# Squared distance of rows: a late pair of x and y, row 7 in PSUM, and other load widths at the end of a stream

## Chip, cores, metric

One core of one Trainium2 chip. The metric is device time in microseconds (us) of one execution. Verdicts count a difference from 2%.

## The reference

```python
x, y: (1024, 4096) float32, normal
return np.sum((x - y) ** 2, axis=-1).astype(np.float32)     # 1024 values
```

Two arrays of 16.8 MB are read, and 4 KB are written.

## The kernel before

Each of 128 partitions holds 8 rows of 4096 columns (row 0 to row 7, columns 0 to 32767). SyncE issues a stream of loads of x and y, which alternate and get smaller toward the end. VectorE subtracts a piece as soon as its y has landed (L175), ScalarE squares and sums it (L181), and VectorE adds the sums of the pieces of a row (`complete`, L188). The last 128 columns of row 3 ("late") have their y loaded after all else. VectorE does these alone: it subtracts, then multiplies and sums in one instruction (L204) that starts from the sum of the rest of row 3. So the last landing asks nothing of ScalarE.

```python
xw = [4096, 12288, 8192, 5472, 1280, 960, 320, 160]
yw = [16256, 8192, 2624, 2784, 1344, 480, 480, 288]
late, last = 128, 192
LATE = 3
halved = (1, 2, 3, 4)                     # pieces of these y loads are cut in two
cut = (LATE + 1) * D - late
# ... cut: xs = plain spans of xw; ys = spans of yw, skipping the late columns
ys += [(N - last, N), (cut, cut + late)]

# ... cut: load(), which gives every load its own semaphore
def square(c0, c1, acc):
    a = X[:, home(c0, c1)]
    nc.scalar.wait_ge(diffs, n["diffs"])
    nc.scalar.activation(out=a, in_=a, func=Square, accum_out=acc).then_inc(acts, 1)
    # ... cut: count of squares (other counters are cut below)

for j, (c0, c1) in enumerate(ys):
    final = j == len(ys) - 1
    wait_loaded(c1, landed_y[j][1])
    for piece in pieces_of(j, c0, c1):
        sub(*piece)
        r = piece[0] // D
        if final:
            nc.vector.wait_ge(diffs, n["diffs"])
            nc.vector.tensor_tensor_reduce(
                out=Y[:, home(*piece)], in0=X[:, home(*piece)], in1=X[:, home(*piece)],
                scale=1.0, scalar=parts_of(r, 1), op0=mult, op1=add,
                accum_out=results[:, r : r + 1]).then_inc(sums, 1)
            continue
        square(*piece, where[piece])
        # ... cut: issue of the second half of the loads when rows 0 and 1 are squared
    if j == 4:
        for r in (4, 5, 6):
            complete(r)
complete(7)
nc.sync.wait_ge(sums, n["sums"])
nc.sync.dma_start(out=ov, in_=results).then_inc(stored, 16)
```

## Time and profile before

| | before |
|---|---|
| time, median of 6 runs | 84.13 us (84.0 to 84.2) |
| span of the profiled run | 82.63 us |
| DMA packets, share of 16 engines | 2736, 95.9% |
| last data moved / last two y seen | 79.8 / 80.05 and 80.25 us |
| last reduce starts / store issued | 80.99 / 81.18 us |

The kernel is a stream of 33.55 MB that keeps the DMA engines full from 2 to 79.8 us, with a tail of 1.4 us of work and 1.45 us of store. The page, the windows at the end of the stream, the timeline of the tail and the chain are shown and read in the prediction below.

### The profile page before, as it was taken

Reading aid. Unit: us, or ns where it says so; the run is one execution under the profiler, and the core shown is the slowest. Engines: PE = TensorE matmul, PEld = TensorE weight load, DVE = VectorE, ACT = ScalarE, POOL = GpSimd, SP = SyncE. Lnnn points to the kernel's source line nnn. Section 1 sums busy time; section 2 is a strip of 40 time slices with the busy share of each in tenths; the row PEclk is TensorE's granted clock in tenths of the full one; section 3 lists DMA queues with packets and bytes.
Section 4 is the critical chain, followed back from the end, with each engine's and each line's share of the span. In section 5 each row is a group of like instructions: output and inputs, shape, how many; then the busy total and the mean of one; then the engine's idle time right before and its main releaser. Section 6 shows DMA issues by size and latency. Waiting matters only on the chain.

```text
span 82.6 us, 136 instructions
## 1 busy us (share of the span) xinstructions
DVE 36.8 (45%) x27; ACT 33.4 (40%) x41; POOL 0.2 (0%) x4
## 2 busy tenths in 40 slices
DVE  0000000000000000000299999999189996989992
ACT  3300000000000000000000979889896999899991
POOL 0000000000000000000000000000000000000000
DMA  5998998888999991999599699969979799999960
GB/s 127 389 500 381 595 547 381 381 381 381 504 504 504 504 504 63 441 504 504 254 508 508 286 476 508 476 286 508 423 339 509 339 437 440 426 402 416 395 220 2
DMA packets 2736, 33.56 MB, mean 406 GB/s; under 512 B 432, under 2 KB 1328, under 8 KB 1712
## 3 DMA queue, kind: packets, MB, share of 16 engines
q1 hardware_dynamic: 2736, 33.56, 95.9%
HBM read 33.55 MB, written 0.00 MB: 406 GB/s over the span
## 4 chain that ended last, share of the span: by engine, by line
DMA 63%; SPq 16%; DVE 12%; ACT 4%; issue 1%
DMA Y<-in_y_dram 63%; SPq L108 16%; DVE X L175 11%; ACT X L181 4%; DVE Y L204 0%; DVE results L188 0%; SPq L220 0%; DVE results L204 0%
## 5 line engine op out<-in xcount | busy, mean ns | idle before, releaser
L175 DVE TENSOR_TENSOR X<-X,Y 128x2048 f32<-128x2048 f32 (+10 forms) x21 | 36.2, 1780 | 44.3 <-DMA Y<-in_y_dram 44.3
L181 ACT ACTIVATE X<-X 128x2048 f32<-128x2048 f32 (+9 forms) x20 | 31.2, 1559 | 46.1 <-DVE X L175 46.0
L181 ACT ACTIVATION_READ_ACCUMULATOR X<-X 128x1 f32 x20 | 3.7, 186 | 0.0
L181 ACT ACT_TABLE_LOAD x1 | 1.3, 1283 | 1.4 <-PEq L19 1.4
L188 DVE TENSOR_REDUCE results<-parts 128x1 f32<-128x2 f32 (+2 forms) x4 | 0.4, 152 | 0.0
L204 DVE CUSTOM_DVE_ANT_0 Y<-X,parts 128x128 f32<-128x128 f32 x1 | 0.4, 352 | 0.0
L250 POOL MEMSET const-bfloat16-1.0<- 128x1 bf16 x1 | 0.1, 101 | 0.0
L250 POOL MEMSET const-uint8-127<- 128x1 uint8 x1 | 0.1, 101 | 0.0
L250 POOL MEMSET const-float32-0.0<- 128x1 f32 x1 | 0.1, 98 | 0.2 <-issue 0.2
L250 POOL MEMSET const-float32-1.0<- 128x1 f32 x1 | 0.1, 98 | 0.0
L204 DVE DVE_READ_ACCUMULATOR2_ANT results<- 128x1 f32 x1 | 0.1, 83 | 0.0
## 6 DMA issues: line engine op xcount, KB each, us to landing
Y<-in_y_dram SPq DMA_DIRECT2D x1, 8128.0 KB, 39.0
X<-in_x_dram SPq DMA_DIRECT2D x1, 6144.0 KB, 20.2
X<-in_x_dram SPq DMA_DIRECT2D x1, 4096.0 KB, 48.3
Y<-in_y_dram SPq DMA_DIRECT2D x1, 4096.0 KB, 57.5
X<-in_x_dram SPq DMA_DIRECT2D x1, 2736.0 KB, 13.3
X<-in_x_dram SPq DMA_DIRECT2D x1, 2048.0 KB, 7.1
Y<-in_y_dram SPq DMA_DIRECT2D x1, 1392.0 KB, 19.0
Y<-in_y_dram SPq DMA_DIRECT2D x1, 1312.0 KB, 16.1
```

The lines of the kernel that those rows point to most:

```text
L108: nc.sync.dma_start(out=dst[:, home(c0, c1)], in_=src[:, c0:c1]).then_inc(sem, 16)
L175: nc.vector.tensor_sub(out=a, in0=a, in1=Y[:, home(c0, c1)]).then_inc(diffs, 1)
L181: nc.scalar.activation(out=a, in_=a, func=Square, accum_out=acc).then_inc(acts, 1)
L188: nc.vector.tensor_reduce(out=results[:, r : r + 1], in_=parts_of(r, len(row_parts[r])), axis=mybir.AxisListType.X, op=add,).then_inc(sums, 1)
L204: nc.vector.tensor_tensor_reduce(out=Y[:, home(*piece)], in0=X[:, home(*piece)], in1=X[:, home(*piece)], scale=1.0, scalar=parts_of(r, 1), ...
L250: nc = _bacc.Bacc("TRN2", target_bir_lowering=False, num_devices=1)
```

## The change

It has three parts. The late piece becomes 96 columns of both x and y, loaded after everything else. The sums of row 7, and the squares of its last eight pieces, go to PSUM, to make ScalarE's last instructions shorter. The widths of the other loads are fitted anew (19 loads instead of 18).

```diff
-    xw = [4096, 12288, 8192, 5472, 1280, 960, 320, 160]
-    yw = [16256, 8192, 2624, 2784, 1344, 480, 480, 288]
-    late, last = 128, 192
+    xw = [4096, 12192, 8192, 5440, 928, 928, 672, 224]
+    yw = [16288, 8192, 2624, 2752, 992, 896, 352, 352, 224]
+    late = 96
-    halved = (1, 2, 3, 4)
+    halved = (1, 2, 3, 4, 5)
 ...
+    def pieces(widths):                  # spans that skip the late columns, then the late piece
+        ...
+    xs, ys = pieces(xw), pieces(yw)
 ...
+    last_parts = nc.alloc_psum_tensor("last_parts", [P, 512], F32).ap()
+    last_squares = nc.alloc_psum_tensor("last_squares", [P, 7 * 512], F32).ap()
+    squares_at = {}                      # the last pieces of row 7, as many as fit
 ...
+        to = squares_at.get((c0, c1), a)
-        nc.scalar.activation(out=a, in_=a, func=Square, accum_out=acc).then_inc(acts, 1)
+        nc.scalar.activation(out=to, in_=a, func=Square, accum_out=acc).then_inc(acts, 1)
 ...
-        wait_loaded(c1, landed_y[j][1])
+        wait_loaded(c1, landed_y[j][1], final)     # the last x is waited for only by the final piece
```

More of the change, by code (lines that the diff above doesn't have):

```diff
@@ L68 @@
     results = nc.alloc_sbuf_tensor("results", [P, R], F32).ap()
-    xw = [4096, 12288, 8192, 5472, 1280, 960, 320, 160]
-    yw = [16256, 8192, 2624, 2784, 1344, 480, 480, 288]
-    late, last = 128, 192
+    xw = [4096, 12192, 8192, 5440, 928, 928, 672, 224]
+    yw = [16288, 8192, 2624, 2752, 992, 896, 352, 352, 224]
+    late = 96
     LATE = 3
-    halved = (1, 2, 3, 4)
+    halved = (1, 2, 3, 4, 5)
     cut = (LATE + 1) * D - late
-    assert sum(xw) == N and sum(yw) == N - late - last
-    xs, c = [], 0
-    for w in xw:
-        xs.append((c, c + w))
-        c += w
-    ys, c = [], 0
-    for w in yw:
-        ys.append((c, c + w))
-        c += w
-        if c == cut:
-            c += late
-    ys += [(N - last, N), (cut, cut + late)]
+    def pieces(widths):
+        spans, c = [], 0
+        for w in widths:
+            spans.append((c, c + w))
+            c += w
+            if c == cut:
+                c += late
+        assert c == N
+        return spans + [(cut, cut + late)]
+    xs, ys = pieces(xw), pieces(yw)
     prog = Program(nc, tc)
@@ L111 @@
     order = []
-    have = 0
-    for c0, c1 in ys:
-        while have < c1:
-            order.append((landed_x, xv, X, "x") + xs[len([o for o in order if o[3] == "x"])])
-            have = order[-1][5]
-        order.append((landed_y, yv, Y, "y", c0, c1))
+    xk = 0
+    for piece in ys:
+        while xk < len(xs) and (xs[xk][0] < piece[1] if xk < len(xs) - 1 else piece == ys[-1]):
+            order.append((landed_x, xv, X, "x") + xs[xk])
+            xk += 1
+        order.append((landed_y, yv, Y, "y") + piece)
     todo = list(order)
@@ L145 @@
     parts = nc.alloc_sbuf_tensor("parts", [P, total], F32).ap()
+    last_parts = nc.alloc_psum_tensor("last_parts", [P, 512], F32).ap()
+    last_squares = nc.alloc_psum_tensor("last_squares", [P, 7 * 512], F32).ap()
+    squares_at = {}
     k = 0
-    for r, p in enumerate(row_parts):
-        for piece in p:
-            where[piece] = parts[:, k : k + 1] if len(p) > 1 else results[:, r : r + 1]
-            k += len(p) > 1
+    for piece in reversed(row_parts[-1]):
+        w = piece[1] - piece[0]
+        if k + w > 7 * 512:
+            break
+        squares_at[piece] = last_squares[:, k : k + w]
+        k += w
     first = {}
@@ L154, with wait_loaded @@
         if len(p) > 1:
-            first[r] = k
-            k += len(p)
+            first[r] = 0 if r == R - 1 else k
+            k += 0 if r == R - 1 else len(p)
     def parts_of(r, m):
-        return parts[:, first[r] : first[r] + m]
+        home_of = last_parts if r == R - 1 else parts
+        return home_of[:, first[r] : first[r] + m]
+    for r, p in enumerate(row_parts):
+        for k, piece in enumerate(p):
+            where[piece] = parts_of(r, len(p))[:, k : k + 1] if len(p) > 1 else results[:, r : r + 1]
     seen_x = [0]
-    def wait_loaded(c1, ysem):
+    def wait_loaded(c1, ysem, final):
         waits = []
-        while seen_x[0] < len(xs) and xs[seen_x[0]][0] < c1:
+        while seen_x[0] < len(xs) - 1 and xs[seen_x[0]][0] < c1:
             waits.append(seen_x[0])
             seen_x[0] += 1
+        if final:
+            assert seen_x[0] == len(xs) - 1
+            waits.append(seen_x[0])
         nc.vector.wait_ge(ysem, 16)
```

## The prediction

> **What bounds the kernel now.** I began with the page: how busy each engine is, what the DMA queue did, and which chain ended last.
>
> ```profile
> DVE 36.8 (45%) x27; ACT 33.4 (40%) x41; POOL 0.2 (0%) x4
> ...
> DMA packets 2736, 33.56 MB, mean 406 GB/s; under 512 B 432, under 2 KB 1328, under 8 KB 1712
> ...
> q1 hardware_dynamic: 2736, 33.56, 95.9%
> ...
> DMA 63%; SPq 16%; DVE 12%; ACT 4%; issue 1%
> ```
>
> Neither compute engine is busy half the span, while the packets of the one queue fill 95.9% of the 16 engines' span. The 4.1% left over is 3.4 us of 82.6: part of it is at the start, the rest at the end, where nothing is left to load. The chain names SyncE for 16%, but that is SyncE pushing issues into a queue that is already full. So this is a stream of 33.55 MB plus a head and a tail. No work that lies beside the stream can shorten it. The change loads the same 33.55 MB, so it can act in two places only: the cost of the packets, and the time from the last bytes to the end. I therefore read the end of the stream next, in the windows view (columns: window, length, busy time and count of VectorE, ScalarE and GpSimd, clock, DMA share, GB/s):
>
> ```profile
> 73.00:75.00 2.00, 1.73 (x3) 2.00 (x4) 0.00 (x0) 1.00 1.02 423
> 78.00:79.00 1.00, 1.00 (x6) 1.00 (x5) 0.00 (x0) 1.00 1.05 382
> 79.00:79.50 0.50, 0.43 (x1) 0.50 (x3) 0.00 (x0) 1.00 1.11 357
> 79.80:80.00 0.20, 0.20 (x1) 0.20 (x2) 0.00 (x0) 1.00 0.04 8
> ```
>
> The rate falls from 423 to 357 GB/s at full share, as the loads become small, and the data ends at about 79.8 us. VectorE and ScalarE have next to no idle time there. The timeline view then shows who finishes when (start, duration, engine, instruction):
>
> ```profile
> 79.58 1.06 DVE L175 TENSOR_TENSOR X<-X,Y 128x288 f32<-128x288 f32 x3 [0.15 <-DMA Y<-in_y_dram]
> ...
> 80.52 0.35 ACT L181 ACTIVATE X<-X 128x192 f32<-128x192 f32 x1
> 80.67 0.35 DVE L204 CUSTOM_DVE_ANT_0 Y<-X,parts 128x128 f32<-128x128 f32 x1
> 80.77 0.19 ACT L181 ACTIVATION_READ_ACCUMULATOR X<-X 128x1 f32 x1
> 80.95 0.08 DVE L204 DVE_READ_ACCUMULATOR2_ANT results<- 128x1 f32 x1
> 80.99 0.16 DVE L188 TENSOR_REDUCE results<-parts 128x1 f32<-128x8 f32 x1
> 81.18 0.35 SPq L232 DMA_DIRECT2D out_dram<-results  x1
> ```
>
> And the pieces of the chain, in order of time (start, duration, what):
>
> ```profile
> 66.94 13.12 DMA Y<-in_y_dram
> 80.05 0.02 issue
> 80.08 0.57 DVE X L175 x2
> 80.65 0.03 issue
> 80.67 0.35 DVE Y L204
> ```
>
> The semaphore of the 192-column y is seen at 80.05. From there two paths run into the last reduce (80.99). VectorE: subtract 192, subtract 128 (it starts at 80.35, as soon as it can, so its load had landed), multiply and sum, read the accumulator. ScalarE: its square of 192 starts at 80.52, only 0.1 after the start of the read of the accumulator before it (80.42), so ScalarE was held by itself and not by VectorE; its own last read ends at 80.77 + 0.19 = 80.96. The two paths meet within 0.04 us. After the reduce (ends 81.15) there are 82.63 - 81.18 = 1.45 us of store, which the change leaves alone. The tail that it can touch is thus 79.8 to 81.15, or 1.35 us: 1.6% of 84.03. Even a free tail would not be 2%.
>
> **What the Trainium skill says.** "ScalarE: Activation LUTs", section "What ACT_TABLE_LOAD costs", gives an activation without pointer operands 186 ns + 0.833 ns per column, and says neighbours overlap by about 93 ns. The trace agrees: 347 ns at 192 columns (346 by the formula), 595 at 480 (586). "Perfetto Trace Analysis", section "Optimizing Scalar/DVE Operations", puts the access overhead of ScalarE at about 93 ns on SBUF and 51 on PSUM, that of VectorE at 60 on SBUF and 125 on PSUM. This kernel has no PSUM operand, so its trace shows only the SBUF side, which agrees: the two 480 squares start 0.59 us apart, which is 0.40 of columns and 0.19 for two overheads, one of the square and one of its accumulator read. "DMA: Bandwidth & Descriptors", section "Specifications", asks for at least 512 B per piece for line rate, below which the DMA reads, modifies and writes. The trace can't tell: its smallest loads are 128 columns, exactly 512 B (the 432 packets under 512 B are the 128 of the store and 304 completions, 19 transfers by 16). "PSUM — Partial Sum Buffer", section "PSUM bank collisions raise a hardware error", forbids two engines on one bank at once; here VectorE reads the sums after a wait for the last square, so none is due.
>
> **The change part by part.**
>
> *Packets.* Loads go from 18 to 19 (9 x and 10 y), so 128 data packets and 16 completions more: 144/16 = 9 per engine. Their cost, from the windows: at 423 GB/s an engine moves 26.4 B per ns; in 79.0 to 79.5, with packets of 128 to 320 columns (about 800 B on average, my estimate), 22.3 B per ns. 800/22.3 - 800/26.4 = 5.6 ns a packet. So 9 x 5.6 = 0.05 us more stream: the data ends at about 79.85.
>
> *Late pieces.* Before, 128 columns of y came after the 192-column y. Now a 96-column x and y, 192 columns in 384 B packets, come after the 224-column y. Sixteen packets per engine at 384/26.4 + 5.6 = 20 ns make 0.32 us; the old 8 of 512 B made 8 x 25 = 0.20. Landing follows the last byte by about 0.45 us: y8's bytes ended about 0.20 before 79.8, and its semaphore came at 80.05. So the new y8 is seen at 79.85 - 0.32 + 0.45 = 79.98, and the last pair at 79.85 + 0.45 = 80.30.
>
> *VectorE path.* By rows, a subtract takes 285 ns at 128, 357 at 192, 459 at 288 and 656 at 480 columns: 1.05 ns a column. So 224 takes 0.39 and 96 takes 0.25. The following one may start 0.087 before the end (736 columns: 923 ns each, two of them in 1.76 us). The 224 runs from 80.00, and VectorE is free for the 96 at 80.30; the late pair is seen at 80.30 + 0.02. So the 96 starts at 80.32, against 80.35 for the old 128. From there to the multiply took 0.32 and takes 0.29 (32 columns less); from the multiply to the reduce also 0.32, now 0.29. Reduce at 80.90 instead of 80.99. **Gain here: 0.09.**
>
> *Reduce.* It now reads 9 sums from PSUM: 125 - 60 = 65 ns more by the skill's figure, an estimate. It ends at 80.90 + 0.16 + 0.065 = 81.13, against 81.15.
>
> *ScalarE path.* The subtract of 224 ends at 80.39; the square starts at 80.43, its accumulator read 0.19 + 0.05 later at 80.67, and ends at about 80.82 (0.19 less the 0.04 of a nearer write). That is ahead of the reduce at 80.90. Eight of the nine squares of row 7 write to PSUM, at about 2 x 42 ns less each, some 0.7 us of ScalarE in all. What it buys at the end is only that ScalarE no longer binds: it would otherwise come with 32 more columns in its last square.
>
> *Before the tail.* The first subtract waits for 16288 columns of x and y instead of 16384 and 16256: 64 less, 32.8 KB, 0.08 us. It starts earlier at 40.8, and so do the squares and SyncE's second set of issues, but those come with transfers still queued (the 8192-column y issued at 2.77 takes 57.5 us to land, to 60.3; SyncE resumes at 53.4). Worth nothing. VectorE has one subtract more, about 0.06 us, in a stretch in which by my sums it waits for loads anyway.
>
> Sum: -0.09 on VectorE's path (the 0.05 of packets is in it already, through the landing at 80.30), +0.065 in the reduce: **-0.02 us** at the end of the reduce. I put a little more on the gain, because ScalarE leaves the path and the halved pieces spread better: **83.95 us**.
>
> **The rivals.**
> 1. *384 B packets are slow.* If read-modify-write doubles the 20 ns, 16 packets cost 0.32 us more and the last pair lands at 80.6: 84.3 us. For it: the skill's threshold. Against: nothing in this trace; only 98 KB are affected.
> 2. *ScalarE was the real bound of the whole tail.* It is 100% busy from 73 to 80, and 0.7 us of it go away. If the chain is really its own, up to 0.3 us could come off: 83.7 us. Against: its squares start within 0.04 to 0.1 us of the end of their subtract, and the last reduce waits for VectorE as well.
> 3. *The PSUM read or the extra wait costs more than reckoned.* The last subtract now waits for two semaphores, x and y, and the reduce crosses to PSUM: up to 0.1 us more, 84.1 us.
> 4. *The queue starves.* SyncE's issues block on a full queue (5.21 us in one of them), and there is one more to push; if the last were pushed late, its 96 columns would come microseconds late. Against: the last issue ends near 73, almost 7 us before the data does. Small.
>
> **Range and chances.** The terms are all below 0.35 us and of either sign, and the three runs of before themselves span 84.0 to 84.2. So 83.65 to 84.3 us, eight in ten. A change of 2% is 1.68 us, more than the whole tail; faster by that 0.5%, slower by that 1.5% (a starved queue or a slower pattern of packets), same 98%.
>
> **What would show it right or wrong.** In the changed profile: packets 2880, of them 704 under 512 B; mean rate and queue share as before; the data over at 79.8 to 79.9; squares of row 7 into PSUM shorter than 186 ns + 0.833 per column by some 40 to 80, and their accumulator reads near 150; the last reduce near 0.22 us, and starting after VectorE's chain and not after ScalarE's; SyncE's store issue at 81.1 to 81.2. A last subtract that waits for DMA until 80.5 or later would show rival 1, a last reduce 0.2 or more earlier rival 2. I would be wrong altogether if the stream itself ran at another rate, since 0.5% of 79 us outweighs all of the above.

## The result, and the profile after

The changed kernel took 84.19 us in the median of 6 runs (84.06 to 84.5), against 84.13 (84.0 to 84.2). The ratio is 1.0011, with a 95% interval of 0.9992 to 1.003: the same. A ratio here is the mean time of one kernel's fast runs over the mean of the other's of the same rounds, so it is not quite the ratio of the medians.

The page of the changed kernel, for its packets, its queue and the new groups on ScalarE and VectorE:

```profile
DMA packets 2880, 33.56 MB, mean 406 GB/s; under 512 B 704, under 2 KB 1216, under 8 KB 1856
...
q1 hardware_dynamic: 2880, 33.56, 96.0%
...
L197 ACT ACTIVATION_READ_ACCUMULATOR X<-X 128x1 f32 x13 | 2.4, 184 | 0.0
...
L197 ACT ACTIVATION_READ_ACCUMULATOR last_squares<-X 128x1 f32 x8 | 1.1, 133 | 0.0
...
L204 DVE TENSOR_REDUCE results<-last_parts 128x1 f32<-128x9 f32 x1 | 0.2, 166 | 0.0
```

Packets and small packets are as counted, 2880 and 704. A read of ScalarE's accumulator takes 133 ns where it goes to PSUM and 184 where it goes to SBUF. The last reduce takes 166 ns although it reads PSUM.

The windows at the end of its stream (window, length, busy time and count of VectorE, ScalarE and GpSimd, clock, DMA share, GB/s):

```profile
79.50:79.80 0.30, 0.30 (x2) 0.26 (x3) 0.00 (x0) 1.00 1.04 293
79.80:80.00 0.20, 0.20 (x1) 0.20 (x1) 0.00 (x0) 1.00 0.43 112
80.00:80.20 0.20, 0.13 (x1) 0.20 (x3) 0.00 (x0) 1.00 0.03 8
```

Before, the window from 79.8 to 80.0 had a share of 0.04. Now it has 0.43: the data ends at 80.0, not at the predicted 79.85. (The unaltered kernel, run again further down, has 1.01 in this window, so this does not yet show that the change is the reason.)

The timeline of the tail (start, duration, engine, instruction):

```profile
80.63 0.36 ACT L197 ACTIVATE last_squares<-X 128x224 f32<-128x224 f32 x1
80.84 0.32 DVE L220 CUSTOM_DVE_ANT_0 Y<-X,parts 128x96 f32<-128x96 f32 x1
80.92 0.13 ACT L197 ACTIVATION_READ_ACCUMULATOR last_squares<-X 128x1 f32 x1
81.08 0.08 DVE L220 DVE_READ_ACCUMULATOR2_ANT results<- 128x1 f32 x1
81.08 0.17 DVE L204 TENSOR_REDUCE results<-last_parts 128x1 f32<-128x9 f32 x1
81.28 0.35 SPq L248 DMA_DIRECT2D out_dram<-results  x1
```

And its chain, in order of time:

```profile
72.33 8.20 DMA Y<-in_y_dram
80.52 0.02 issue
80.54 0.27 DVE X L190
80.81 0.02 issue
80.84 0.32 DVE Y L220
```

The late pair is seen at 80.52. The last subtract starts at 80.54, 0.19 after the 80.35 of before. The multiply follows 0.30 after it instead of 0.32 (-0.02), and the reduce 0.24 after the multiply instead of 0.32 (-0.08, of which 0.04 is a wait for ScalarE that is gone: the reduce now starts with VectorE's own read of its accumulator, and before it started 0.04 after it). From reduce to store it is 0.20 instead of 0.19. The sum is +0.10, which is the 81.28 - 81.18 of the two store issues. So the tail did get shorter after the last landing, and the last landing came later by more than that.

The trace also holds each of the 16 increments that a load makes on its semaphore, one from each DMA engine. They were sorted for every load. VectorE waits for the last of the 16; the median of them, called the middle engine below, is freer of a straggler.

```
                spread of the 16   middle engine, last y   last of 16,  run,
                first   last load  minus first x           last y       profiled us
before           0.23     0.24      73.12                   80.25        83.96
after            0.38     0.43      73.31                   80.52        84.06
```

Of the 0.27 us between 80.25 and 80.52, 0.17 is the middle engine (80.15 to 80.32) and 0.10 a wider spread of the 16. That spread is there at the first load, which is the same 4096 columns of x in both kernels. In the trace of before, no two increments of the last y come closer than 13 ns, which is 0.20 us for 15 steps, so 0.24 us is nearly as even as that load gets. Whether these 0.27 us belong to the change or to the run is the question of the experiments.

### The profile page after: what moved, and what is told of

Its sections match the earlier page's. It is cut to its first block, busy times and chain, and to the rows that moved or that the text cites. A ratio compares the mean times of both kernels' runs of the same rounds, so it can differ in the third digit from the quotient of the medians.

```text
span 82.7 us, 141 instructions
## 1 busy us (share of the span) xinstructions
DVE 37.0 (45%) x28; ACT 33.5 (40%) x43; POOL 0.2 (0%) x4
## 2 busy tenths in 40 slices
DMA packets 2880, 33.56 MB, mean 406 GB/s; under 512 B 704, under 2 KB 1216, under 8 KB 1856
## 3 DMA queue, kind: packets, MB, share of 16 engines
q1 hardware_dynamic: 2880, 33.56, 96.0%
## 4 chain that ended last, share of the span: by engine, by line
DMA 57%; SPq 23%; DVE 11%; ACT 4%; issue 1%
DMA Y<-in_y_dram 57%; SPq L109 23%; DVE X L190 11%; ACT X L197 4%; DVE Y L220 0%; DVE results L204 0%; SPq L236 0%; DVE results L220 0%
## 5 line engine op out<-in xcount | busy, mean ns | idle before, releaser
L190 DVE TENSOR_TENSOR X<-X,Y 128x2048 f32<-128x2048 f32 (+11 forms) x22 | 36.4, 1705 | 44.2 <-DMA Y<-in_y_dram 44.0
L197 ACT ACTIVATE X<-X 128x2048 f32<-128x2048 f32 (+5 forms) x13 | 27.0, 2075 | 46.0 <-DVE X L190 46.0
L197 ACT ACTIVATE last_squares<-X 128x448 f32<-128x448 f32 (+5 forms) x8 | 4.2, 534 | 0.1
L197 ACT ACTIVATION_READ_ACCUMULATOR X<-X 128x1 f32 x13 | 2.4, 184 | 0.0
L197 ACT ACTIVATION_READ_ACCUMULATOR last_squares<-X 128x1 f32 x8 | 1.1, 133 | 0.0
```

Of the source, the lines that this page charges most:

```text
L190: nc.vector.tensor_sub(out=a, in0=a, in1=Y[:, home(c0, c1)]).then_inc(diffs, 1)
L197: nc.scalar.activation(out=to, in_=a, func=Square, accum_out=acc).then_inc(acts, 1)
```

## The experiments

Theory: the three parts are each worth less than 0.1 us at the end. PSUM takes away the 0.04 us wait for ScalarE, the late pair brings the end of the stream later because its packets are small, and the rest is chance of the run. Rivals: one part gains and another gives it back at a size that shows; packets under 512 B are slow by a factor; 19 loads spread the engines more than 18. The first four ran on one chip, the next four on a second, the last two on a third; each was timed in five rounds. The record names no chip for the traces of before and after, so two traces of one kernel may come from two chips.

### The changed kernel again

No edit.

> The changed kernel unaltered, to see how far its tail repeats. Theory (the late pair of x and y lands later because it brings more and smaller packets, and this eats the shorter work): the last subtract again waits for its load and starts at 80.5 to 80.6 us in the profile, the last reduce at 81.05 to 81.15, time 84.1 to 84.2, within 0.2% of the kernel before. Rival (the late landing in the one profile was chance): the last subtract starts at 80.3 to 80.4, the reduce at 80.9, time 83.9 to 84.0.

84.17 us, ratio to before 1.0005 [0.9992, 1.0018]; the profiled run 84.32. The last subtract began at 80.82 and the reduce at 81.35, later than either side expected. The middle engine was where it had been (73.30 after the first load's landing, against 73.31), but the 16 were 0.70 us apart at the first load and 0.72 at the last. The windows of this run show the straggler, a trickle after the stream has ended:

```profile
79.80:80.00 0.20, 0.20 (x2) 0.16 (x2) 0.00 (x0) 1.00 0.31 85
80.00:80.20 0.20, 0.20 (x1) 0.20 (x1) 0.00 (x0) 1.00 0.09 23
80.20:80.40 0.20, 0.12 (x1) 0.20 (x3) 0.00 (x0) 1.00 0.02 6
```

So one kernel's last landing moves by 0.27 us (80.52 to 80.79) between two runs, with nothing changed. A share of 0.02 in a window is a third of one engine out of 16; 15 of the 16 increments had come by 80.49 and the last came at 80.79, so that one engine sets the time of the profiled run.

### PSUM taken out of the changed kernel

```diff
-    last_parts = nc.alloc_psum_tensor("last_parts", [P, 512], F32).ap()
+    last_parts = nc.alloc_sbuf_tensor("last_parts", [P, 512], F32).ap()
-        squares_at[piece] = last_squares[:, k : k + w]
```

> The changed kernel with the sums and squares of row 7 back in SBUF, all else as changed. Theory (PSUM spares ScalarE about 0.08 us per piece, and without it ScalarE would be last with its square of 224 columns): ScalarE's last accumulator read ends at about 81.2 to 81.3 instead of 81.05, the last reduce starts 0.1 to 0.25 us later than in the changed kernel, time 0.1 to 0.2 us longer. Rival (the late landing alone holds the end): the reduce starts at 81.1 as before, time the same within 0.05 us.

84.17 us, 1.0004 [0.999, 1.0019]: the time of the rival. The tail:

```profile
80.77 0.37 ACT L196 ACTIVATE X<-X 128x224 f32<-128x224 f32 x1
80.98 0.32 DVE L219 CUSTOM_DVE_ANT_0 Y<-X,parts 128x96 f32<-128x96 f32 x1
81.05 0.19 ACT L196 ACTIVATION_READ_ACCUMULATOR X<-X 128x1 f32 x1
81.23 0.08 DVE L219 DVE_READ_ACCUMULATOR2_ANT results<- 128x1 f32 x1
81.27 0.16 DVE L203 TENSOR_REDUCE results<-last_parts 128x1 f32<-128x9 f32 x1
```

ScalarE ends at 81.05 + 0.19 = 81.24, and the reduce starts at 81.27, 0.04 after VectorE's read, where in the changed kernel the two start together. The reduce is 0.19 later than in the changed kernel, but 0.15 of that is the landing of this run (80.67 against 80.52). PSUM is worth 0.04 us in this pair of traces, not the 0.1 to 0.25 expected. By shapes, between these two kernels: the square of 480 columns takes 586 ns into SBUF and 572 into PSUM, that of 352 takes 488 and 468, the accumulator read 186 and 133, and the reduce of nine sums 164 from SBUF and 166 from PSUM.

### PSUM alone, on the kernel before

```diff
+    last_parts, last_squares = ...       # as in the change
+            if r == R - 1:
+                where[piece] = last_parts[:, i : i + 1]
-        nc.scalar.activation(out=a, in_=a, ...
+        nc.scalar.activation(out=squares_at.get((c0, c1), a), in_=a, ...
```

> The kernel before with only the sums and squares of row 7 put in PSUM. Theory (there ScalarE and VectorE tie at the last reduce): ScalarE's last accumulator read ends 0.1 us earlier or more, VectorE's chain does not move, the reduce starts at 81.0 as before, time the same within 0.05 us. Rival (ScalarE alone bounds the tail): the reduce starts 0.1 to 0.3 us earlier, time 83.8 to 84.0.

84.14 us, 1.0006 [0.9987, 1.0025]. The lines that answer to the tie of before:

```profile
80.88 0.13 ACT L195 ACTIVATION_READ_ACCUMULATOR last_squares<-X 128x1 f32 x1
81.09 0.08 DVE L218 DVE_READ_ACCUMULATOR2_ANT results<- 128x1 f32 x1
81.09 0.16 DVE L202 TENSOR_REDUCE results<-last_parts 128x1 f32<-128x8 f32 x1
```

ScalarE ends at 81.01 and is free 0.08 before the reduce; the 0.04 us between VectorE's read and the reduce are gone here as well. The time is the theory's, and the rival that ScalarE alone bounds the tail does not hold. But VectorE's chain did move, against the theory: the last y was seen at 80.39 instead of 80.25, and the reduce started at 81.09 instead of 81.0. And the wait for ScalarE can vanish without PSUM: the kernel before, run again below, shows 0.01 us of it. So this run shows the shorter accumulator read (186 ns to 128), and not that PSUM took the wait away.

### Only y late in the changed kernel

```diff
-    xw = [4096, 12192, ...
+    xw = [4096, 12288, ...               # xs as plain spans, 18 loads
-    if final: waits.append(the last x)
```

> The changed kernel, but the late 96 columns of x come with the 12288-column load, so that only y is late: 18 loads instead of 19. Theory: the last load lands 0.1 to 0.25 us earlier against the y of 224 columns before it, the last subtract starts right after that of 224 columns (80.3 to 80.45), the end comes 0.05 to 0.15 us earlier unless the y of 224 columns lands that much later, because only half as many bytes follow it. In that case ScalarE's square of 224 is last. Rival (late x costs nothing, a slow stretch of the stream does): the last subtract starts at 80.5 as in the changed kernel.

84.24 us, 1.0011 [0.9994, 1.0027]. The 224-column y was seen 0.19 us later on the middle engine than in the changed kernel (80.13 against 79.94) and the late y at the same time (80.31 against 80.32), with 18 loads instead of 19. The last subtract came right after that of 224 columns, as expected, but not earlier. The reduce started at 81.24, 0.05 after VectorE's read at 81.19, because ScalarE ended at 81.21: with x not late, the square of 224 columns is last even with PSUM. In these two traces, then, the late x moves the y before it forward and leaves the end where it is; the null test further down shows how little one trace can be trusted with such a difference.

### The late pair at 32, 128 and 256 columns

```diff
-    xw = [4096, 12192, ...];  yw = [16288, ...];  late = 96
+    xw = [4096, 12256, ...];  yw = [16352, ...];  late = 32
# and 12160, 16256, 128;  and 12032, 16128, 256
```

> The changed kernel with a late pair of 32 columns instead of 96, packets of 128 B. Read on the engine in the middle of the 16 that make up a landing, as the time between the landing of the late x and of the late y. Theory (a packet below 512 B costs no less than one of 512 B, about 24 ns, as the 96-column loads showed with 0.19 us): gap 0.18 to 0.20 us. Rival (bytes at 26.4 B per ns plus 5.6 ns a packet): gap 0.08 to 0.10 us. Work after the last landing is 0.13 us shorter than with 96 columns, yet ScalarE's square of 224 comes to bind, so the time stays within 0.1 us of the changed kernel under either.

> The changed kernel with a late pair of 128 columns, packets of 512 B. Theory (no penalty above a common floor for packets up to 512 B): gap between the landings of late x and late y 0.19 to 0.21 us on the middle engine, the last landing on that engine as with 96 columns within 0.05 us; last subtract and multiply 0.07 us longer together; time 0.0 to 0.1 us above the changed kernel. Rival (packets under 512 B are read, modified and written at twice the cost): the last landing comes 0.1 to 0.3 us earlier than with 96 columns, time up to 0.2 us shorter.

> The changed kernel with a late pair of 256 columns: the late work made large on purpose. Both theories of packets: gap 0.34 to 0.38 us. Theory (the chain after the last landing is the end of the kernel, column by column): the last subtract takes 0.42 us and the multiply 0.49, together 0.33 us more than with 96 columns, and the time is 0.25 to 0.4 us above the changed kernel, 84.4 to 84.6 us. Rival (something else ends the kernel, ScalarE or the store): less than 0.1 us more.

```
late columns (bytes)   late x to late y,   last y minus first x,   time, ratio to before
                       middle engine       middle engine
 32 (128)              0.19 us             73.55                   84.41  1.0029 [1.0018, 1.0041]
 96 (384)              0.17 to 0.20        73.29 to 73.31          84.19  1.0011; again 84.17  1.0005
128 (512)              0.19                73.32                   84.15  1.0005 [0.9993, 1.0016]
256 (1024)             0.32                73.28                   84.46  1.0038 [1.0026, 1.005]
```

(The row of 96 holds the changed kernel, its repeat, and the one without PSUM.) The landings of the late x and y are the same 0.19 us or so apart with 32, 96 or 128 columns, and no less for a quarter of the bytes. As to landings, the theory of a common floor holds. The rival of bytes plus 5.6 ns a packet would have had 0.08 to 0.10 at 32 columns. The rival of a doubled cost under 512 B would have had the 128 columns land 0.1 to 0.3 us earlier than the 96. Neither came.

That the floor is a cost of the packets (24 ns each, 8 on an engine) is not shown, though. The same traces hold a record of every packet, and there a late packet takes 13 ns at 128 B, 22 at 384, 27 at 512 and 46 at 1024. The starts agree: from the mean start of the 256 packets of 896 B to that of the 256 late packets behind them it is 0.40, 0.47, 0.51 and 0.65 us, a distance in which half of an engine's 16 late packets lie. That makes a packet of 128 B 9 ns shorter than one of 384 B, close to the 10 ns that the rival's formula gives. (All packets of a size have the same duration, so the profile may model these times.) A cause that no run separates from the packets is the increments themselves: in the seven traces with a late pair, no two increments of the late x came closer than 13 ns, and none of the late y closer than 11, and 15 such steps are 0.17 to 0.20 us. Some other loads have increments 2 to 3 ns apart.

The 32 columns missed in time: 0.22 to 0.24 us above the two medians of the changed kernel, where less than 0.1 was expected. Two terms are visible. The pair does not land closer together for its fewer bytes: 64 columns less of x and of y go to the large loads, 2 x 64 x 512 B = 65.5 KB, which take 0.155 us at the 423 GB/s of the stream, while the late x and y are still 0.19 us apart. The middle engine's landing was 0.24 later. And ScalarE became last: its read ended at 81.44, and the reduce started at 81.48, 0.09 after VectorE's read. How much of the rest is chance of the run stays open.

The 256 columns came as expected in time, 0.27 to 0.29 above the changed kernel; their gap of 0.32 is below the expected 0.34 to 0.38. The subtract took 0.43 and the multiply 0.48. This is the control: of 0.33 us more work after the last landing, nearly all is paid. The 128 columns came 0.02 to 0.04 below the changed kernel instead of 0.0 to 0.1 above it, which is within the noise.

### The late pair alone, on the kernel before

```diff
-    xw = [4096, 12288, ...
+    xw = [4096, 12160, ...               # and xs.append((cut, cut + late)), issued before the last y
```

> The kernel before with only its late 128 columns of x split off as a 19th load after the 192-column y, all in SBUF as before. Theory (one more load lengthens the stream by 9 descriptors per engine): the last landing, on the middle engine and counted from the first load's landing, comes 0.05 to 0.15 us later than the 73.12 us of the kernel before, the y of 192 columns about 0.1 to 0.15 us earlier; time 0.0 to 0.15 us above the kernel before. Rival (the spread of the 16 engines is larger with 19 loads than with 18): the spread at the last landing is 0.4 us or more here and grows during the stream. Against it: in all six traces so far the spread at the first load already equals that at the last within 0.2 us, so I expect it to be set there, by chance of the run, here as well.

84.14 us, 1.0002 [0.999, 1.0014]. The 16 engines were 0.57 us apart at the first load and 0.60 at the last, and between 0.57 and 0.61 at every load: the spread did not grow in the stream. That it is chance of the run is not shown. Over all twelve traces the spread at the first load is 0.23 to 0.44 us in the five with 18 loads and 0.38 to 0.70 in the seven with 19, so a link with the number of loads stays open; in the time of this run it cost nothing that can be seen. The middle engine's last landing came 73.19 us after the first, against 73.12, and that of the 192-column y 0.12 earlier, as expected; the next run shows that this difference is too small to mean anything.

### The kernel before again

No edit.

> The kernel before unaltered, as a null test. Theory (how far the 16 engines lie apart is set at the first load by chance of the run): the spread at the first landing differs from the 0.23 us of the first trace, anywhere from 0.2 to 0.7 us, stays within 0.2 us of itself to the last landing, and the last subtract shifts with it, so that the profiled time lies between 84.0 and 84.4. Ratio to itself 1.000 within 0.15%. Rival (the kernel before owes its even engines to its loads): spread 0.23 us within 0.03 again, and 84.0 us.

84.18 us, ratio to itself 1.0012 [0.9983, 1.0041], single runs from 84.01 to 84.67. The spread was 0.23 us at the first load again and 0.27 at the last, so for this kernel the rival's spread came true, by chance or not. The time did not follow: the profiled run took 84.18, not 84.0, and the middle engine's last landing came 73.48 us after the first, 0.36 later than in the first trace. The stream fell behind in its second half: counted in the same way, the x of 5472 columns landed at 59.82 instead of 59.63. So the stream itself differs between two traces of one kernel by more than any part of the change was seen to move it, and an uneven start of the engines is only one of two ways in which the end can move. The lines that answer to those of the changed kernel:

```profile
79.80:80.00 0.20, 0.20 (x1) 0.20 (x2) 0.00 (x0) 1.00 1.01 296
...
81.20 0.08 DVE L204 DVE_READ_ACCUMULATOR2_ANT results<- 128x1 f32 x1
81.21 0.16 DVE L188 TENSOR_REDUCE results<-parts 128x1 f32<-128x8 f32 x1
81.40 0.35 SPq L232 DMA_DIRECT2D out_dram<-results  x1
```

The last y was seen at 80.48 and the store issued at 81.40, against 80.52 and 81.28 in the first trace of the changed kernel. The unaltered kernel thus shows nearly the whole 0.27 us by which the changed one seemed to land later. And the wait for ScalarE is down to 0.01 us without PSUM.

### The widths alone

The changed kernel without PSUM (the edit above), with only y late and 128 columns of it.

> The last part alone: the widths of the changed kernel, but everything in SBUF and only y late, with 128 columns. Theory (each part moves the end by less than 0.1 us): the last landing, middle engine, counted from the first load's, at 73.1 to 73.25 us; ScalarE is last, because its square of 224 columns takes 0.03 us more than one of 192 and nothing spares it; reduce 0.04 us or more after the read of VectorE's accumulator; time 84.1 to 84.25 us. Rival (the refit is what gains, and the late x gives it back): time under 84.0 us.

84.29 us, 1.002 [1.0000, 1.0039], 0.04 above the expected range. The middle engine's last landing came at 73.33, above the expected 73.1 to 73.25, but below the 73.48 of the kernel before in the same rounds. ScalarE was last, as expected: VectorE's read started at 81.25 and the reduce at 81.31, 0.06 later. The rival that the widths gain is out; whether they cost a few hundredths can't be told from a null ratio of 1.0012.

## Why the prediction was right

"Same" and the range (83.65 to 84.3, measured 84.19) were right. The reason given for "same" held best: the kernel is a stream, and the part of the tail that can change is smaller than 2%. That the number came within 0.24 us is in part luck: at the end of the reduce, predicted at 81.13 and measured at 81.25, a landing 0.22 later was partly made up by a shorter way from multiply to reduce (-0.05) and a reduce without the PSUM surcharge (-0.06). The steps:

1. *The kernel is a DMA stream with a tail.* Right. Share of the queue 95.9% and 96.0%, the same 406 GB/s.
2. *The two paths of the tail meet within 0.04 us, and PSUM takes ScalarE off.* The tie is right. PSUM's part rests on one pair of traces: the wait of 0.04 us is gone in the changed kernel and came back when PSUM was taken out of it. But it was also gone in the kernel before when that ran again without PSUM (0.01), and with only y late ScalarE was last by 0.05 in spite of PSUM. Which path ends last thus varies by hundredths of a us from trace to trace. The prediction also left the 0.04 in its 0.29 from multiply to reduce; 0.24 was measured.
3. *Packets 2880, 704 small.* Right. Their cost, "384/26.4 + 5.6 = 20 ns", is close to the 22 ns of the packet records. The gap from the 224-column y to the late y, predicted 0.32 us, was 0.34 by the last increments (80.18 to 80.52) and 0.38 on the middle engine (79.94 to 80.32); where the difference arises is open.
4. *The late pair is seen at 80.30.* Wrong by 0.22 (80.52). Nearly all of it was there before the pair: the 224-column y was seen at 80.18 instead of 79.98, and the pair added 0.34 instead of 0.32. What failed is the end of the data (79.85) and the landing, which the prediction took as a fixed 0.45 us behind the data, both from the one trace of before. The landing holds the spread of 16 engines, 0.24 us in that run and 0.43 in this, and a stream that differs by up to 0.36 us between runs of one kernel. The step took one run's landing for a constant.
5. *The reduce pays 65 ns for PSUM.* Wrong: 166 ns against 164 with the same nine sums. The squares into PSUM were also expected 40 to 80 ns shorter, and were 4 to 24; the accumulator read, expected near 150 ns, took 133.
6. *The sum is -0.02 us, "I put a little more on the gain", 83.95.* The sum was nearer than the adjustment: 84.03 - 0.02 = 84.01, and no gain came. There was no measured reason for the 0.06 more.
7. *Rivals.* Rival 1 (slow 384 B packets) has no doubling to show, neither in the landings nor in the packet records. Its sign, a last subtract at 80.5 or later, did come, at 80.54 and 80.82; but the kernel before moved its own last landing from 80.25 to 80.48, so the sign could not tell the rival from the run. Rival 2 (ScalarE the bound of the whole tail) is out: no run with PSUM was faster. Of rival 3, the PSUM read costs nothing. Rival 4 (a starved queue) did not show: the late y was issued by 73.3 us, 7 us before it landed, and it landed in step with the loads ahead of it.

What stays open: the true difference of the two kernels. Their ratios, 1.0011 and 1.0005, lie inside what the kernel before shows against itself (1.0012), so a difference of 0.05 us either way can't be told, nor whether the late pair delays the last landing at all. No part beat the kernel before, and no combination of parts suggested itself that would.

## What to carry to other kernels

When a stream of loads sets the time, bound the gain first: only the work after the last landing is for sale, and here the control of 256 columns shows that more of it is paid nearly in full, while no rearrangement of the last loads brought the time under that of the kernel before. Here a last load of 128 or 384 B to a partition landed no sooner after the load before it than one of 512 B, so cutting the last piece finer than that won nothing. What sets this floor is not known. And before reading 0.1 us out of two profiles, run one kernel twice: here the last landing of one kernel moved by 0.2 to 0.3 us in the profile with nothing changed.

## What the Trainium skill lacked or had wrong

- "DMA: Bandwidth & Descriptors", section "Specifications": it asks for 512 B or more and speaks of read-modify-write below. The runs show no jump there. By landings there is a floor: 0.17 to 0.20 us between two loads of 128 partitions at 128, 384 and 512 B alike, 0.32 at 1024 B. By the packet records the time goes down with the bytes, 13, 22 and 27 ns at 128, 384 and 512 B. What the engine does below 512 B no run shows.
- "Perfetto Trace Analysis", section "Optimizing Scalar/DVE Operations": its figures (93 to 51 ns for ScalarE, 60 to 125 for VectorE, which it says appear about doubled in a profile) carried over in part only. Squares into PSUM were 4 to 24 ns shorter (612 to 608 at 512 columns, 488 to 468 at 352), the accumulator read 53 ns shorter (186 to 133), and a VectorE reduce of nine elements took 166 ns from PSUM and 164 from SBUF.
- "DMA: Bandwidth & Descriptors", section "Why a DMA increments its semaphore by 16 and not by 1": it says that the engines finish independently, but not how far apart, nor how close two increments can come (13 ns at the closest for some loads, 2 to 3 for others, much the same in all twelve traces). In these twelve traces the 16 increments of the first load lie 0.23 to 0.70 us apart, and those of the last load 0.23 to 0.72; in ten of them the two differ by 0.07 us at most.
- No page has the scatter of a full stream: the middle engine's last landing, 73 us after the first, differed by 0.36 us between two runs of one kernel.
